# Low parts of the weight tiles in the tail: GpSimd in eight pieces, two tiles on VectorE

## The chip, the cores and the metric

One core of a Trainium2 chip runs the whole program. The time is device microseconds (us) of one execution; the median of several runs is compared. Engines by the profile's names: PE (TensorE, matmuls), DVE (VectorE), ACT (ScalarE), POOL (GpSimd), SP (SyncE, which issues nearly all DMAs).

## The reference

A fused model of two blocks in float32, sequence length 256, width 1024. The first block is one hybrid layer (attention and spatial gating, then 16 experts that choose their tokens) and a norm. The second block has two layers, an even one (sliding-window and latent attention, 8 heads each) and an odd one (16 heads with forget gates, FOX below). Cut to what the tail of the kernel computes:

```
x = rmsnorm(xl + gt2 * expert_choice_ffn(...), g_final)      # end of the first block

def mla_swa_layer(x, positions, g_in, w_in, ...):
    h = rms_norm(x, g_in)
    z = h @ w_in
    cq, ckv, kpe, q_s, k_s, v_s, gate = split_cols(z, EVEN_SPLITS)
    ...                                    # 8 latent heads, 8 sliding-window heads
    o = jnp.concatenate([o_mla, o_swa], axis=-1)
    return x + (o * jax.nn.silu(gate)) @ w_out

def fox_layer(x, g_in, w_in, b_f, w_out):
    h = rms_norm(x, g_in)
    q, k, v, f_logit, gate = split_cols(h @ w_in, ODD_SPLITS)
    ...                                    # 16 heads, causal, with cumulated log gates
    return x + (o * jax.nn.silu(gate)) @ w_out
```

## The kernel before

The program is one core's list of instructions per engine, in the order in which the code is written (a manual schedule); each engine runs its list in that order, and waits where an instruction needs another engine's result.

**Weights and slots.** A weight tile is 128 x 2048 float32 (1 MB): 256 columns of a weight matrix, with the eight blocks of 128 rows (k = 0 to 7) side by side, 256 columns each. The tiles lie in a fixed number of slots of SBUF. `get(i)` gives tile i, `done(i)` frees its slot, and each freed slot makes `pump()` (L254) issue the next load on SP, in one fixed order.

**Split products.** In the tail every product is made of three matmuls on float32r operands, `mm3` (L141 to L145): high by high, high by low, low by high. `split(i, n, eng, parts)` (L154 to L167) makes the two parts of a weight tile: ScalarE casts the tile (hi, L162), and GpSimd (G) or VectorE (V) subtracts, lo = t − hi (L163). Tables of letters say which engine takes which tile: `ORD_SPLITS` for the five input tiles k, c, v, q and r, `TAIL_SPLITS` for all others of the tail. In the tail GpSimd has c, q, r, all four tiles each of the even layer's gates (g) and output weights (o), and eight of the FOX layer's tiles. Its instruction is one per tile; q's is in two halves, c is 1664 wide.

**End of the first block.** While the last expert's second product runs, `ORD` interleaves it with the input tiles of the even layer, and `stats` collects sums of squares into p_st. Then come the inverse norms on VectorE: ms4 and r4 by L1459 to L1462 and `rsqrt` (L180 to L192: an integer estimate and three Newton steps), and rr at L1464. After that a string, `REST = "cBqtQ"`, sets the order: `latent_out` (c), then for B two `bc_rows` (TensorE spreads a column over the partitions into p_bc, L1340, and VectorE copies it, L1342) and `keys_out` (L1478, L1481), then q's product is finished (q), a transpose (t), and `q_out(0)` (Q, L1499), which scales the first queries. `q_out(1)` for tile r runs inside the pipeline.

**The attention pipelines.** `pipeline` runs over pairs of heads, 4 sliding-window and 4 latent ones: `soft_a` makes the scores (p_s) and the exponentials (L1361 on VectorE, L1365 on ScalarE), `soft_n` divides (`V.tensor_scalar`, L1380, four per pair), `soft_b` transposes (p_pt, L1387; copies L1390 and L1392), `soft_c` multiplies with the values and gates the result (og L1445, ogh L1446, ogl L1447). A table `fills` puts other work between these: the gate products (p_gate, L1436 to L1439), the transposes p_hT (L1602), the splits of the g and o tiles (`ESP` sets their places), and `eo_part`, the output product (p_eo), for the tiles o0 to o3. The odd layer has a second such pipeline over 8 pairs with its own fills (k scaled at L1762, bias L1841, p_oo).

Of the kernel before, what the change touches and what calls it, by code (L numbers as in the profile page):

```python
# [14 lines left out]
OP = mybir.AluOpType  # L15
# [14 lines left out]
ORD_SPLITS = "VGVGG"  # L30
# [6 lines left out]
PARTS = (1, 1, 2, 2, 1)  # L37
# [25 lines left out]
def body(ctx, tc, x, c, ctx_in, c_ctx, w_mod, b_mod, g_mix, g_ffn, w_in, q_gain, k_gain, v_gain,  # L63
# [4 lines left out]
    PE, V, S, G = nc.tensor, nc.vector, nc.scalar, nc.gpsimd  # L68
# [16 lines left out]
    def slot(name, weight=False):  # L85
        if not weight:
            keep[0] = max(keep[0] - 1, 0)
        if not slots_free:
            raise RuntimeError("slots: " + " ".join(v[3] for v in owner.values()))
        n = next((n for n in slots_free if weight or n not in slow), slots_free[0])  # L90
        slots_free.remove(n)
        slow.discard(n)
        t = big.tile([128, 2048], F32, name=name, tag="B%d" % n)
        owner[id(t)] = (slots_free, n, t, name)
        return t
# [14 lines left out]
    def free(*ts):  # L110
        for t in ts:
            q, n, _, _ = owner.pop(id(t))
            q.append(n)
        pump()
# [14 lines left out]
    def small(name, shape, dt=F32, bufs=2):  # L129
        return work.tile(list(shape), dt, name=name, tag="sm_" + name, bufs=bufs)  # L130
# [4 lines left out]
    def mm(o, lhsT, rhs, start, stop):  # L135
        PE.matmul(o, lhsT, rhs, start=start, stop=stop, skip_group_check=True)  # L136

    def r_(ap):
        return ap.bitcast(F32R)
# [14 lines left out]
    def split(i, n=2048, eng=None, parts=1):  # L154

        t = get(i)
        hi, lo = slot("hi"), slot("lo")
        if eng is None:
            eng = dict(G=G, V=V)[TAIL_SPLITS[i - qup_i + 5]]
        for a in range(parts):  # L160
            c_ = slice(n * a // parts, n * (a + 1) // parts)
            S.copy(r_(hi[:, c_]), t[:, c_])  # L162
            eng.tensor_tensor(r_(lo[:, c_]), t[:, c_], hi[:, c_], op=OP.subtract)  # L163
        if i >= qup_i:
            limit[0] = max(limit[0], i + AHEAD[i - qup_i + 5])
        done(i)
        return hi, lo  # L167
# [82 lines left out]
    def pump(upto=-1):  # L250
        while len(tiles) <= min(limit[0], len(loads) - 1) and len(slots_free) > (0 if len(tiles) <= upto else keep[0]):
            t = slot("w%d" % len(tiles), True)
            for view, src in loads[len(tiles)]:
                nc.sync.dma_start(view(t), src)  # L254
            tiles.append(t)

    def get(i):
        if i >= len(tiles):
            limit[0] = max(limit[0], i)
            pump(i)  # L260
        return tiles[i]

    def done(*idx):
        free(*[tiles[i] for i in idx])
# [43 lines left out]
    e_i, E_COLS = {}, {"k": 928, "q": 416, "r": 672}  # L308
    for e in range(NEXP):
# [7 lines left out]
        else:  # L317
            for ch in ORD:
# [6 lines left out]
                else:  # L325
                    n, a2 = int(ch) // 2, int(ch) % 2
# [211 lines left out]
    W = {}  # L538
# [29 lines left out]
    for nm, g in (("q", qg), ("k", kg)):  # L568
        t = small("rows_" + nm, (128, 256), bufs=1)
# [8 lines left out]
    qr = qr_.rearrange("p (b h a d) -> p b h a d", b=2, h=8, a=2)  # L578
# [359 lines left out]
    for m2 in range(4):  # L938
        w = W.pop("o%d" % m2)
# [157 lines left out]
    def between(e):  # L1097

        def f(z, k):
            if z == 1 and k == 0 and e == 0:  # L1100
                index_columns()
                hold(6)
                tables()
            if z == 1 and e + 1 < NEXP and k in (2, 4, 6):
                (pick, fetch, turn)[k // 2 - 1](e + 1)
        return f


    def hidden(e):

        hp, xe, before = [], xes.pop(e), between(e)
        for z in range(2):
            p = bank("p_h%d" % z)
            for k in range(8):
                before(z, k)
                t = get(exp_i[e][z][k]).rearrange("p (a j m) -> p a j m", a=4, j=4)
                lhs = xe[:, 32 * k:32 * k + 32]
                for j in range(4):
                    mm(p[32 * j:32 * j + 32, :].rearrange("p (a m) -> p a m", a=4), lhs, t[:, :, j, :], k == 0, k == 7)
                done(exp_i[e][z][k])  # L1120
            hp.append(p)
        s1 = w2k("s1")
        S.activation(s1, hp[0], AF.Silu)
        hid = w2k("hid")
        V.tensor_tensor(hid, s1, hp[1], op=OP.mult)  # L1125
        free(*hp)
        hidT = w2k("hidT").rearrange("p (a s) -> p a s", a=16)
        for a in range(4):
            V.transpose(hidT[:, 4 * a:4 * a + 4, :], hid[:, 128 * a:128 * a + 128].rearrange("p (r q) -> p q r", q=4))  # L1129
        oh4 = w2k("oh4", 256)  # L1130
        V.tensor_scalar(r_(oh4), trow, ig4[:, e:e + 1], None, op0=OP.is_equal)
        return hidT, oh4
# [111 lines left out]
    def freer(key):  # L1244
        return lambda: free(*W.pop(key))

    hidT, oh4 = hidden(NEXP - 1)
    sqs = [small("rows_" + c_, (128, 256), bufs=1) for c_ in "qk"]
    steps, accs, reach = deque(), {}, {}
# [35 lines left out]

    for ch in ORD:
        if ch in e_i:
            W[ch] = split(e_i[ch], 1664 if ch in "cv" else 2048, dict(G=G, V=V)[ORD_SPLITS["kcvqr".index(ch)]],
                          PARTS["kcvqr".index(ch)])
            if ch == "v":  # L1290
                if have < 8:
                    more("c")
            elif have < 8:
                product(ch)
            continue
        n, a2 = int(ch) // 2, int(ch) % 2
        if a2 == 0:
            yp = bank("p_y")
        busy(BUSY[int(ch)])
        i = exp_i[-1][2][int(ch)]  # L1300
        t = get(i)
        for z in range(2):
            for q in range(4):
                mm(yp[32 * q:32 * q + 32, 0:256], hidT[:, 8 * a2 + 4 * z + q, :],
                   t[:, 1024 * z + 256 * q:1024 * z + 256 * q + 256], a2 == 0 and z == 0, a2 == 1 and z == 1)
        done(i)
        if a2 == 0:
            some(STEPS[n])
            continue
        ys = gated(NEXP - 1, yp[:, 0:256], 256)  # L1310
        free(yp)
        flush()
        some(STEPS[4 + n])
        p = bank("p_sc")
        for i in range(2):
            for mi in range(2):
                mm(p[:, 256 * mi:256 * mi + 256], r_(ys[i][:, 128 * mi:128 * mi + 128]), r_(oh4),
                   i == 0 and mi == 0, i == 1)
        for mi in range(2):
            m = 2 * n + mi  # L1320
            add_to_x(m, p[:, 256 * mi:256 * mi + 256])
            scaled(y1h[:, m, :], y1l[:, m, :], xT[:, m, :], gfe[:, m:m + 1])
            add_squares(m)
        free(p)
        flush()
        some(STEPS[8 + n])
        have = 2 * n + 2
        for c_ in accs:
            more(c_)
        for m in {2: (5,), 3: (6, 7)}.get(n, ()):  # L1330
            steps.append(lambda m=m: stats(m))
# [5 lines left out]
    def bc_rows(col2, name):  # L1337
        p = bank("p_bc")
        for b in range(2):
            PE.transpose(p[:, 128 * b:128 * b + 128], col2[:, b:b + 1].to_broadcast([128, 128]), ident)  # L1340
        t = small(name, (128, 256), bufs=1)
        V.tensor_copy(t, p[:, 0:256])  # L1342
        free(p)
        return t
# [118 lines left out]
    rsqrt(r4, ms4, 4)  # L1463
    V.tensor_tensor(rr, r4[:, 2:4], r1, op=OP.mult)  # L1464
    free(p_st)
    zt_, qst_ = slot("zt"), slot("qst")
    zn = zt_[:, 0:832].rearrange("p (b n) -> p b n", b=2)
    vsn = zt_[:, 832:1088].rearrange("p (b n) -> p b n", b=2)
# [7 lines left out]
    def keys_out():  # L1476
        p = finish("k")
        V.tensor_tensor(vT, p[:, 256:512], rb, op=OP.mult)  # L1478
        for v_ in range(2):
            for a in range(2):  # L1480
                V.tensor_tensor(ksT[64 * a:64 * a + 64, v_, :], p[64 * v_:64 * v_ + 64, 0:256],  # L1481
                                rb[64 * v_:64 * v_ + 64, :], op=OP.mult)
        free(p)
        freer("k")()
# [19 lines left out]
    for ch in REST:  # L1504
        if ch == "B":
            r1b = bc_rows(r1, "rows_q")
            rb = bc_rows(rr, "rows_k")
            keys_out()
        elif ch == "c":
            latent_out()  # L1510
        elif ch == "q":
            finish("q")
        elif ch == "Q":
            q_out(0)
        elif ch == "r":
            product("r")
            some(3)
        elif ch == "t":
            p = bank("p_vT")
            for b in range(2):  # L1520
                PE.transpose(p[:, 128 * b:128 * b + 128], vT[:, 128 * b:128 * b + 128], ident)
            S.copy(zt_[:, 832:1088], p[:, 0:256])
            free(p)
# [387 lines left out]
    for b in range(2):  # L1911
        ss = s4[:, 2 * b:2 * b + 2]
        v, u, r, y, z, rf = (s2[:, 6 * b + i:6 * b + i + 1] for i in range(6))
# [45 lines left out]
```

## Time and profile before

| | us |
|---|---|
| median of 3 runs | 1377.9 (1374.32 to 1378.91) |
| profiled execution, own time | 1375.06 |
| its span | 1373.3 |
| PE busy | 1082.7 (79%) |
| DVE busy | 466.8 (34%) |
| ACT busy | 266.0 (19%) |
| POOL busy | 113.4 (8%) |

Busy shares are means over the whole span. The first three quarters stream the experts' weights; the input tiles of the even layer, and all that the change is about, come in the last quarter, which is called the tail here. "Idle" and "waits" are read for one engine at a time: the time in which it stands, and the instruction whose end let it go on.

### The profile page before, as it was taken

The numbers are of one execution on the slowest core, as the hardware profiler recorded it, in microseconds if no ns is written. First come the engines' busy times: TensorE is split into PE (matmuls) and PEld (weight loads), VectorE is DVE, ScalarE is ACT, GpSimd is POOL, SyncE is SP. The second block draws the span as 40 slices with busy tenths as digits, with TensorE's granted clock in tenths as the row PEclk, the third lists the DMA queues.
The fourth block names the chain that finished last, engine by engine and source line by source line (L and its number), as shares of the span: only waits on it lengthen the run. The fifth ranks groups of instructions, "written<-read, shape, count | busy, mean of one in ns | idle before, by whom it ended". The sixth has DMA issues, their size and how long they took to land.

```text
span 1373.3 us, 16868 instructions
## 1 busy us (share of the span) xinstructions
PE 1082.7 (79%) x6827; PEld 521.8 (38%) x6827; DVE 466.8 (34%) x1167; ACT 266.0 (19%) x537; POOL 113.4 (8%) x65
## 2 busy tenths in 40 slices
PE   6999987777767777776766767777776979899988
PEld 3875932111211111111111211111120667799887
DVE  3747542111201111121111112111120668867984
ACT  3437310000000000000000000000000536545453
POOL 2000100000000000000000000000000332560420
PEclk9999999997979789897888989788896999999999
DMA  9995799999999999999999999999999952381320
GB/s 374 400 400 229 287 387 426 427 426 426 427 427 426 427 427 427 427 427 427 427 426 427 426 426 427 427 427 427 427 427 408 362 182 82 107 290 64 123 93 32
DMA packets 114685, 482.76 MB, mean 352 GB/s; under 512 B 8010, under 2 KB 61520, under 8 KB 63152
## 3 DMA queue, kind: packets, MB, share of 16 engines
q1 hardware_dynamic: 113504, 479.10, 85.4%
q0 software_dynamic: 848, 2.48, 0.6%
q8 instruction: 54, 0.88, 0.2%
q14 instruction: 23, 0.19, 0.0%
q10 hardware_dynamic: 256, 0.10, 0.0%
HBM read 480.59 MB, written 1.06 MB: 351 GB/s over the span
## 4 chain that ended last, share of the span: by engine, by line
DMA 64%; PE 24%; DVE 9%; ACT 2%; issue 1%; ACTq 0%; SPq 0%; DVEq 0%
DMA w<-in_w_dram 63%; PE p_aT L136 4%; PE p_aN L136 3%; PE p_gate L136 2%; PE p_out L136 2%; PE p_oo L136 2%; PE p_mod L136 1%; PE p_eo L136 1%; PE p_aF L136 1%; DVE pr L1380 1%; PE p_s L136 1%; PE p_o L136 1%; PE p_y L136 1%; DVE pr L1361 1%; DVE lo L163 1%
## 5 line engine op out<-in xcount | busy, mean ns | idle before, releaser
L136 PE MATMUL p_y<-w,hidT 128*32 128x512 f32 (+1 forms) x1088 | 237.9, 628 | 65.8 <-DMA w<-in_w_dram 48.8
L136 PE MATMUL p_h<-w,rows_k 128*32 128x512 f32 x1024 | 177.8, 770 | 87.4 <-DMA w<-in_w_dram 87.4
L136 PE MATMUL p_h<-w,rows_q 128*32 128x512 f32 x1024 | 172.9, 753 | 87.2 <-DMA w<-in_w_dram 85.7
L163 POOL TENSOR_TENSOR lo<-w,hi 128x2048 fp32r<-128x2048 f32 (+2 forms) x20 | 86.7, 4340 | 1005.7 <-DVE hidT L1129 903.9
L136 PEld LDWEIGHTS p_y<-w,hidT 128*32 128x32 f32 x1088 | 54.9, 116 | 253.6 <-issue 144.6
L1139 DVE SCALAR_TENSOR_TENSOR ysl<-p_y,ig,ysh 128x512 fp32r<-128x512 f32 (+1 forms) x34 | 24.4, 719 | 262.1 <-ACT ysh L1138 260.6
L136 PEld LDWEIGHTS p_h<-w,rows_k 128*32 128x32 f32 x1024 | 25.7, 119 | 206.3 <-DMA w<-in_w_dram 178.6
L136 PEld LDWEIGHTS p_h<-w,rows_q 128*32 128x32 f32 x1024 | 25.5, 119 | 201.1 <-DMA w<-in_w_dram 170.5
L1041 DVE TENSOR_SCALAR oh<-p_ix,cst,rs 128x32 f32<-128x32 f32 x30 | 7.9, 306 | 265.9 <-PE p_ix L136 265.9
L1138 ACT ACTIVATE ysh<-p_y,ig 128x512 fp32r<-128x512 f32 (+1 forms) x34 | 22.4, 662 | 388.8 <-PE p_y L136 388.8
L1062 ACT COPY xr<-p_g 64x256 f32<-64x256 f32 x16 | 5.8, 365 | 432.2 <-PE p_g L136 227.7
L162 ACT CAST hi<-w 128x2048 fp32r<-128x2048 f32 (+3 forms) x44 | 75.0, 1729 | 23.6 <-DMA w<-in_e_w_in_dram 19.2
L163 DVE TENSOR_TENSOR lo<-w,hi 128x2048 fp32r<-128x2048 f32 (+2 forms) x24 | 47.7, 2005 | 23.3 <-ACT hi L162 22.1
L1143 DVE SCALAR_TENSOR_TENSOR xT<-p_sc,m,xT 128x256 f32<-128x256 f32 x128 | 51.8, 475 | 4.0 <-PE p_sc L136 4.0
L1125 DVE TENSOR_TENSOR hid<-s,p_h 128x512 f32<-128x512 f32 x16 | 11.0, 687 | 95.0 <-PE p_h L136 95.0
L1063 DVE COPY xr<-p_g 64x256 f32<-64x256 f32 x16 | 6.7, 416 | 94.1 <-ACT xr L1062 94.1
L136 PE MATMUL p_aT<-y2h,hi 128*128 128x256 f32 x128 | 36.7, 287 | 0.0
L136 PE MATMUL p_aT<-y2h,lo 128*128 128x256 f32 x128 | 36.3, 284 | 0.2 <-POOL lo L163 0.2
L136 PE MATMUL p_aT<-y2l,hi 128*128 128x256 f32 x128 | 36.3, 284 | 0.1
L136 PE MATMUL p_g<-yn,oh 128*32 128x512 f32 x128 | 34.6, 660 | 0.4 <-DVE oh L1008 0.4
L1365 ACT ACTIVATE pr<-pr,st 128x128 f32<-128x128 f32 x64 | 28.5, 448 | 32.1 <-DVE st L1361 32.1
L1380 DVE TENSOR_SCALAR pr<-pr,st 128x128 f32<-128x128 f32 x64 | 27.4, 491 | 0.6
(488 smaller groups left out, 1783.4 us busy)
## 6 DMA issues: line engine op xcount, KB each, us to landing
w<-in_w_dram SPq DMA_DIRECT2D x376, 1024.0 KB, 19.6
w<-in_w_mod_dram SPq DMA_DIRECT2D x24, 1024.0 KB, 11.1
w<-in_o_w_in_dram SPq DMA_DIRECT2D x16, 1024.0 KB, 7.8
w<-in_w_dram SPq DMA_DIRECT2D x16, 512.0 KB, 8.0
w<-in_w_in_dram SPq DMA_DIRECT2D x7, 1024.0 KB, 17.3
w<-in_e_w_in_dram SPq DMA_DIRECT2D x7, 1024.0 KB, 9.8
w<-in_w_out_dram SPq DMA_DIRECT2D x4, 1024.0 KB, 9.4
w<-in_e_w_out_dram SPq DMA_DIRECT2D x4, 1024.0 KB, 10.7
```

Source lines behind the costliest of these rows:

```text
L136: PE.matmul(o, lhsT, rhs, start=start, stop=stop, skip_group_check=True)
L162: S.copy(r_(hi[:, c_]), t[:, c_])
L163: eng.tensor_tensor(r_(lo[:, c_]), t[:, c_], hi[:, c_], op=OP.subtract)
L1041: V.tensor_scalar(oh[b], p[:, 0:n], table(C_TCOL + b, 1), rs2[:, b:b + 1], op0=OP.is_equal, op1=OP.mult)
L1063: V.tensor_copy(t[:, 256:512], p[0:64, 256:512])
L1125: V.tensor_tensor(hid, s1, hp[1], op=OP.mult)
L1138: S.activation(r_(h), yp, AF.Copy, scale=g)
L1139: V.scalar_tensor_tensor(r_(l), yp, g, h, op0=OP.mult, op1=OP.subtract)
L1143: V.scalar_tensor_tensor(xT[:, m, :], p, gt2[:, m:m + 1], xT[:, m, :], op0=OP.mult, op1=OP.add)
L1361: V.tensor_tensor_reduce(t[:, c0:c1], sp[:, c0:c1], bb[b], scale, init, OP.add, OP.min, st[:, 2 * z + b:2 * z + b + 1])
L1365: S.activation(t[:, c0:c1], t[:, c0:c1], AF.Exp, bias=st[:, 2 * z + b:2 * z + b + 1], scale=-1.0, accum_out=st[:, 4 + 2 * z + b:5 + 2 * z ...
L1380: V.tensor_scalar(t[:, c0:c1], t[:, c0:c1], st[:, 8 + 2 * z + b:9 + 2 * z + b], None, op0=OP.mult)
```

## The change

In `split`, a tile whose low part is GpSimd's is now subtracted in eight instructions of an eighth of the columns each (256, and 208 for c), so that each is one of the eight k blocks of the tile; VectorE's low parts stay whole. For the last two input tiles, q and r, a new function `split_late` casts both in halves on ScalarE and puts their low parts (two halves each, now VectorE's) and the `done` of the tile into lists. These are called later: q's first half behind rr, its second half and `done` between the two copies of `bc_rows` and `keys_out`, and r's two halves and `done` behind `keys_out`.

```diff
@@ split
-            eng.tensor_tensor(r_(lo[:, c_]), t[:, c_], hi[:, c_], op=OP.subtract)
+            w = n // 8 if eng is G else n // parts
+            for b in range(c_.start, c_.stop, w):
+                d_ = slice(b, b + w)
+                eng.tensor_tensor(r_(lo[:, d_]), t[:, d_], hi[:, d_], op=OP.subtract)
@@ new
+    lows = {"q": [], "r": []}
+
+    def split_late(i, low):
+
+        t, hi, lo = get(i), slot("hi"), slot("lo")
+        for a in range(2):
+            c_ = slice(1024 * a, 1024 * a + 1024)
+            S.copy(r_(hi[:, c_]), t[:, c_])
+            low.append(lambda c_=c_: V.tensor_tensor(r_(lo[:, c_]), t[:, c_], hi[:, c_], op=OP.subtract))
+        low.append(lambda: done(i))
+        return hi, lo
+
@@ for ch in ORD
-            W[ch] = split(e_i[ch], 1664 if ch in "cv" else 2048, dict(G=G, V=V)[ORD_SPLITS["kcvqr".index(ch)]],
-                          PARTS["kcvqr".index(ch)])
+            if ch in "qr":
+                W[ch] = split_late(e_i[ch], lows[ch])
+            else:
+                W[ch] = split(e_i[ch], 1664 if ch in "cv" else 2048, dict(G=G, V=V)[ORD_SPLITS["kcvqr".index(ch)]],
+                              PARTS["kcvqr".index(ch)])
@@ behind rr
     free(p_st)
+    lows["q"].pop(0)()
@@ for ch in REST, "B"
             rb = bc_rows(rr, "rows_k")
+            for f in lows["q"]:
+                f()
             keys_out()
+            for f in lows["r"]:
+                f()
```

The list of VectorE before, from the last step of the inverse norms to the first scaled queries (rs_t and r are the rsqrt's, rows_q and rows_k the spread columns, vT and zt the keys and values, qst the queries):

```order
L191 SCALAR_TENSOR_TENSOR rs_t_5517<-r_5510,rs_u_5516 128x1 x4
L192 SCALAR_TENSOR_TENSOR r_5510<-rs_t_5517,r_5510 128x4
L1464 TENSOR_TENSOR rr<-r_5510 128x2
L1342 COPY rows_q<-p_bc 128x256
L1342 COPY rows_k<-p_bc 128x256
L1478 TENSOR_TENSOR vT<-p_aT,rows_k 128x256
L1481 TENSOR_TENSOR zt<-p_aT,rows_k 64x256 x4
L1499 SCALAR_TENSOR_TENSOR qst<-p_aT,slope,rows_k 128x256 x2
```

The same stretch of VectorE's list after the change (w_5196 is tile q, w_5202 tile r):

```order
L194 SCALAR_TENSOR_TENSOR rs_t_5522<-r_5515,rs_u_5521 128x1 x4
L195 SCALAR_TENSOR_TENSOR r_5515<-rs_t_5522,r_5515 128x4
L1482 TENSOR_TENSOR rr<-r_5515 128x2
L1258 TENSOR_TENSOR lo<-w_5196,hi 128x1024
L1360 COPY rows_q<-p_bc 128x256
L1360 COPY rows_k<-p_bc 128x256
L1258 TENSOR_TENSOR lo<-w_5196,hi 128x1024
L1497 TENSOR_TENSOR vT<-p_aT,rows_k 128x256
L1500 TENSOR_TENSOR zt<-p_aT,rows_k 64x256 x4
L1258 TENSOR_TENSOR lo<-w_5202,hi 128x1024 x2
L1518 SCALAR_TENSOR_TENSOR qst<-p_aT,slope,rows_k 128x256 x2
```

Four low parts of 1024 columns have come in between rr and the first scaled queries; the rest stands as it stood.

GpSimd's list before, from the last sums of squares of the first block on (w_5718, w_5724 and w_5726 are the first tiles of the pipeline, the last line is a small load of the FOX layer's gate weights):

```order
L1242 TENSOR_TENSOR rows_k<-rows_k,sq 128x256
L163 TENSOR_TENSOR lo<-w_5196,hi 128x1024 x2
L163 TENSOR_TENSOR lo<-w_5202,hi 128x2048
L163 TENSOR_TENSOR lo<-w_5718,hi 128x2048
L163 TENSOR_TENSOR lo<-w_5724,hi 128x2048
L163 TENSOR_TENSOR lo<-w_5726,hi 128x2048
L1684 DMA wf<-in_o_w_in_dram 128x8x32
```

And after (w_5727, w_5740 and w_5742 are the same three tiles under new numbers):

```order
L1245 TENSOR_TENSOR rows_k<-rows_k,sq 128x256
L166 TENSOR_TENSOR lo<-w_5727,hi 128x256 x8
L166 TENSOR_TENSOR lo<-w_5740,hi 128x256 x8
L166 TENSOR_TENSOR lo<-w_5742,hi 128x256 x8
L1707 DMA wf<-in_o_w_in_dram 128x8x32
```

q's and r's low parts are gone from GpSimd's list, and each tile behind them is eight instructions; the order of the tiles is the same. The lists of PE and SP keep their order, and ScalarE's has r's cast in two halves.

## Rows read from the trace of the kernel before

**Rows 1.** Busy time by stretch: from:to, length, each engine's busy us, clock, DMA.
```profile
1109.30:1112.30 3.00, 3.00 (x16) 3.00 (x15) 2.87 (x7) 2.16 (x10) 0.00 (x0) 0.50 1.09 385
1200.00:1279.00 79.00, 78.87 (x665) 75.71 (x664) 56.33 (x115) 37.07 (x60) 28.69 (x13) 1.00 0.54 181
```

The columns of this view: us, then busy time of PE, PEld, DVE, ACT and POOL with the count of instructions, the granted clock as a share of full speed, the share of DMA, GB/s.

**Rows 2.** What TensorE waited for in the tail: us in total, times, longest.
```profile
PE p_bc L1340 <- DVE r L192: 7.3, 1, 7.3
PE p_eo L136 <- ACT ogh L1446: 4.8, 1, 4.8
PE p_s L136 <- DVE k L1762: 2.5, 1, 2.5
PE p_pt L1387 <- DVE pr L1380: 2.4, 1, 2.4
PE p_gate L136 <- DVE lo L163: 1.7, 1, 1.7
```

**Rows 3.** The chain of waits round the inverse norms: start us, us, what.
```profile
1097.36 1.81 DVE ms L1462
1099.19 2.32 DVE r L180
1101.58 4.39 DVE r L182
...
1108.54 1.11 PE p_bc L1340 x4
1109.65 7.43 PE p_aT L136 x48
...
1117.64 0.93 PE p_s L136 x8
```

**Rows 4.** VectorE's timeline ahead of these: start us, us, instruction.
```profile
1096.96 0.17 DVE L1460 RECIPROCAL rr<-ms 128x2 f32<-128x2 f32 x1
1097.16 0.16 DVE L1461 SCALAR_TENSOR_TENSOR ms<-rr,p_st 128x2 f32<-128x2 f32 x1
```

**Rows 5.** GpSimd's timeline, with the idle time before and what ended it.
```profile
1082.84 0.73 POOL L1242 TENSOR_TENSOR rows_k<-rows_k,sq 128x256 f32<-128x256 f32 x1
1083.54 0.91 POOL L1242 TENSOR_TENSOR rows_q<-rows_q,sq 128x256 f32<-128x256 f32 x1
1084.40 0.73 POOL L1242 TENSOR_TENSOR rows_k<-rows_k,sq 128x256 f32<-128x256 f32 x1
...
1096.68 9.25 POOL L163 TENSOR_TENSOR lo<-w,hi 128x1024 fp32r<-128x1024 f32 x3 [5.01 <-ACT hi L162]
...
1181.68 9.29 POOL L163 TENSOR_TENSOR lo<-w,hi 128x2048 fp32r<-128x2048 f32 x2 [7.99 <-DVE st L1361]
```

**Rows 6.** VectorE's L1215 beside such a sum, and later without one.
```profile
1082.89 0.96 DVE L1215 SCALAR_TENSOR_TENSOR y1l<-xT,gfe,y1h 128x256 fp32r<-128x256 f32 x1 [0.62 <-ACT y1h L1214]
...
1093.82 0.48 DVE L1215 SCALAR_TENSOR_TENSOR y1l<-xT,gfe,y1h 128x256 fp32r<-128x256 f32 x1 [0.22 <-ACT y1h L1214]
```

**Rows 7.** The chain of waits in the pipelines of both layers.
```profile
1139.45 4.29 DVE pr L1380
...
1145.37 2.83 PE p_hT L1602 x16
...
1152.92 1.88 PE p_hT L1602 x16
...
1193.56 9.21 PE p_eo L136 x56
...
1209.54 5.96 PE p_eo L136 x48
...
1302.04 2.29 DVE lo L163
...
1309.43 6.79 PE p_aN L136 x48
```

**Rows 8.** ScalarE's cast of tile o3 in its timeline.
```profile
1199.36 1.91 ACT L162 CAST hi<-w 128x2048 fp32r<-128x2048 f32 x1 [4.35 <-POOL lo L163]
```

## The prediction

> **What bounds the kernel now.** I first read the table of waits of the matmul engine over the tail [rows 2]. Before the tail the kernel loads the experts' weights, and the change touches nothing there that anybody waits for. In the tail TensorE is the engine to look at: in the 79 us from 1200 it is busy 78.87 us [rows 1], although GpSimd does 28.69 us of low parts beside it. A delay of another engine costs time only where TensorE stands for it, and the table names the five long stands: 7.3, 4.8, 2.5, 2.4 and 1.7 us, 18.7 us together. These, and matmuls that run slower after such a stand, are all that can be won in the tail.
>
> Next I asked the chain of waits what makes DVE late [rows 3]. Three operations on a few elements each take 1.81, 2.32 and 4.39 us: L1462, L180 and L182, all arithmetic from SBUF to SBUF. The reciprocal among them takes 0.17 us and L1461, which reads PSUM, 0.16 [rows 4]. The timeline of GpSimd holds the reason: low parts of the q and r tiles run there from 1096.68 for 9.25 us [rows 5], and the last long DVE operation ends at 1105.97, within 0.05 us of the end of the last of them. An operation of DVE whose data are in SBUF, other than a reciprocal, stands until the GpSimd operation ends. At 1139.45 L1380 takes 4.29 us on the chain [rows 7], which is about the length of one whole tile of GpSimd: two take 9.29 [rows 5].
>
> The Trainium skill, page "SBUF — State Buffer", section "Who interferes with whom", says that DVE and GpSimd share one pair of ports, which one instruction holds exclusively until it ends. The three norm operations agree. The same rule speaks against pieces: a GpSimd operation that already waits may take the ports after every single DVE operation. That is rival A, which is priced from rows below.
>
> **Part 1: the low parts of q and r leave GpSimd and go behind the norms.** Removed: three GpSimd operations, and with them the three stands. At 0.17 us instead of 1.81, 2.32 and 4.39 the norms end 8.52 − 0.51 = 8.0 us earlier. p_bc now starts at 1108.54 [rows 3], and rr is there a moment later, at about 1108.7; then 1100.7. TensorE stood 7.3 us for it [rows 2], so that it can begin p_bc right behind p_lat, at 1101.2. Having stood, it ran the q product (48 matmuls) in 7.43 us [rows 3], while 48 of the same shape later take 5.96 [rows 7]; the granted clock just behind the stand is 0.50 of full speed, the lower level of 1.2 GHz [rows 1]. Without the stand I take 5.96: q would end at 1101.2 + 0.55 (four p_bc at full clock, half their 1.11 us [rows 3]) + 5.96 = 1107.7.
>
> Added on DVE, ahead of the q_out that releases the first attention pair: four halves of 1024 columns. A tile of 2048 takes DVE 2.29 us [rows 7], so a half is 1.15. DVE: rr at 1100.7; q's first half to 1101.85; copies and keys_out (7 operations in 2.87 us [rows 1], the halves between them) and q's second half to 1105.9; r's halves to 1108.2. (TensorE wants q's second half in the middle of the product, at 1104.7; it is there at about 1103.9.) With some 0.1 us for the waits among them q_out begins at 1108.3. Now p_s starts at 1117.64, which is 0.56 us behind the end of the q product at 1109.65 + 7.43 [rows 3]; these 0.56 us are the first half of q_out, so that p_s comes at about 1108.85. TensorE alone would have allowed 1107.7 + 0.56 = 1108.25. So DVE is what ends last here, and the term is **−8.8 us**. The bounds are 0, if something that the trace doesn't show holds q_out, and −9.4. The q tile's weight slot comes free some 2 us later than now, and r's likewise; the loads that take these slots are for tiles of the pipeline that are used much later, so I take nothing for it, and D holds the other case. GpSimd is empty until its next tile, and loses nothing.
>
> **Part 2: eight pieces.** Sixteen tiles of 2048 columns (and c, early, where nobody waits) are written in pieces of 256. Such a piece was already in the trace, as the sums of squares of 128x256: they start 0.70 us apart, and the one beside a DVE operation takes 0.91 [rows 5]. So a tile takes 8 × 0.70 = 5.6 us instead of 4.65, or 8 × 0.87 = 7.0 with a DVE operation in each gap. On the other side L1215 took 0.96 us beside the pieces and 0.48 alone [rows 6]: a stand of half a microsecond where a whole tile would cost four. Nothing else is added: TensorE waits for pieces instead of tiles, which lets it begin on the first of the eight k steps earlier.
>
> What that is worth, stand by stand:
> - p_pt behind L1380: TensorE stood 2.4 us [rows 2], and of the transposes behind it 16 took 2.83 us against 1.88 for as many later [rows 7], so at most 3.35. The four operations of L1380 now each wait for a piece at worst; I take **−2.6**.
> - p_eo behind ogh: 4.8 us [rows 2]. Then 56 matmuls took 9.21 us where 48 at full clock take 5.96, which is 6.95 for 56, so 2.25 us more are in it [rows 7]; at most 7.0. But the lead of GpSimd's queue goes here. It has four tiles in a row, o0 to o3. At 0.75 us a piece, nearer to the lone one, o0 and o1, which start at 1181.68 [rows 5], end 16 × 0.75 = 12.0 us later at 1193.7; o2 at 1199.7; the cast of o3, which stood 4.35 us for o2's low part and takes 1.91 [rows 8], at 1201.6; and the first piece that TensorE wants of o3 is the fifth, at 1205.4. TensorE began o3 at 1209.54 [rows 7] and would now want it 7.0 earlier, at 1202.5, which is 2.9 us too soon. (What parts 1 and this list move before it moves both alike.) I take **−4.0**.
> - p_s behind k (L1762), in the second layer: 2.5 us [rows 2], and the 48 matmuls of p_aN after it 6.79 instead of 5.96 us [rows 7], at most 3.3. DVE meets two whole tiles of GpSimd just before; I take **−2.6**.
> - p_gate behind a low part of DVE: 1.7 us [rows 2]; I take **−1.2**.
> - Elsewhere, as from 1200 to 1279, TensorE has no idle time to give back [rows 1]: 0.
>
> **Sum.** −8.8 − 2.6 − 4.0 − 2.6 − 1.2 = −19.2 us, against the profiled execution's own 1375.06 us: 1355.9. That execution lies 2.84 us below the median of the runs, 1377.9, so I add these: **1358.7 us**.
>
> **Rivals.**
> A. *The engines alternate operation by operation.* Where DVE has one operation after the other in the same place, each may wait for a whole piece. L1215 stood 0.48 us for one; at up to 0.56 us eight pieces stop DVE 4.5 us a tile, as much as one operation does now. For it: a GpSimd piece stretched to 0.91 shows that both engines hand over at each end [rows 5, 6]. Against it: reciprocals and operations on PSUM pass [rows 4], and many of DVE's in these stretches are of this kind. Then only part 1 remains: 1377.9 − 8.8 = 1369.1.
> B. *Everything closes.* All stands and their slow matmuls go: 9.4 + 3.35 + 7.0 + 3.3 + 1.7 = 24.75, so 1353.1. For it: og comes earlier, so that ScalarE's casts do as well. Against it: the queue of o0 to o3 as worked out.
> C. *Slower: GpSimd becomes the bound in o0 to o3.* With a piece every p us, the fifth piece of o3 ends 29p + 1.9 us after the start of o0 (24 pieces, a cast, 5 pieces). TensorE wanted it 27.9 us after it, at 1209.54 − 1181.68. This eats the 8.8 us of part 1 and 4.1 more where 29p + 1.9 = 27.9 + 12.9, from p = 1.34 on, if the other stands also stay; at p = 1.5 it is 1377.9 − 8.8 + 17.5 = 1386.6. The rows have 0.70 alone and 0.87 beside DVE [rows 5]; it would take a DVE operation of 0.6 us in each gap.
> D. *No difference*, within 0.3%, about 4 us, which is roughly what a measurement of this kernel can tell from no change: the halves on DVE or a late load hold q_out by half of what is won, and A holds for the rest: about 1375.
>
> **How the numbers follow.** Part 1 hangs on nothing but removing the three stands, and what DVE has to do instead is priced by operations of the same size; part 2 hangs on how the two engines interleave. I give my forecast 0.53, A 0.22, B 0.15, D 0.05, C 0.05. The forecast, B and nearly all of A are faster by over 0.3%: 0.90 faster, 0.05 the same, 0.05 slower. The range goes from 1349, below B by the scatter of the runs of before, to 1370, just above A; outside are C, D and the edge of A and B.
>
> **What the profile would show.** Part 1 is right if L1462, L180 and L182 take about 0.2 us each, p_bc follows p_lat without a stand, and the first p_s starts some 9 us earlier. If p_s waits for q_out and q_out for r's halves, the order on DVE is the bound, as I say. Part 2 is right if L1380 and L1447 stay under 1 us in a stretch with pieces, and if pieces start 0.7 to 0.9 us apart; A shows as stands of about 0.5 us at nearly every DVE operation there, C as a new wait of p_eo for GpSimd's low part. A wait of p_eo of more than 6 us for o3, or a time over 1370, would make the forecast wrong.

## The result

The changed kernel takes 1355.9 us (median of four runs, 1352.65 to 1357.06) where the kernel before takes 1378.4 beside it: 0.9845 of it, 95% interval 0.982 to 0.9869. The profiled execution took 1356.19 us against 1375.06, 18.9 us less.

Where these 18.9 us lie is read from the matmuls of the two traces. I cut the tail at five of them: the first p_lat of the last, uninterrupted stretch of 24; the first p_s; the end of the first gate product behind the first p_o; the first p_f; the end of the third p_aN product of the odd layer; and the last matmul. The front is all that comes ahead of the first cut. All are us worked out from starts and ends in the traces.

| kernel | front | norms and q: to p_s | first pairs: to gate end | output product: to p_f | odd layer: to p_aN end | rest | whole tail |
|---|---|---|---|---|---|---|---|
| before | 1096.40 | 21.24 | 34.42 | 80.80 | 83.37 | 50.72 | 270.54 |
| changed | 1096.25 | 12.16 | 36.41 | 75.73 | 78.78 | 48.78 | 251.87 |
| difference | −0.15 | −9.08 | **+1.99** | −5.07 | −4.59 | −1.94 | −18.67 |
| forecast | 0 | −8.8 | −2.6 | −4.0 | −2.6 | −1.2 | −19.2 |

The sum came out and one of its terms did not. The waits of TensorE in the tail of the changed kernel show it, beside [rows 2]:

```profile
PE p_hT L1625 <- DVE st L1379: 3.0, 1, 3.0
PE p_eo L136 <- DVE ogl L1465: 1.3, 1, 1.3
...
PE p_s L136 <- DVE qst L1518: 0.7, 1, 0.7
...
PE p_eo L136 <- POOL lo L166: 0.3, 1, 0.3
PE p_pt L1405 <- DVE pr L1398: 0.2, 1, 0.2
```

p_bc, p_s behind k and p_gate are gone from the list, and p_eo stands 1.3 us instead of 4.8. But p_hT, which waited for nothing long before, now stands 3.0. (TensorE "stands" while it waits for another engine.)

VectorE's timeline round the inverse norms (start us, us, instruction) answers to the chain in [rows 3]:

```profile
1096.81 0.17 DVE L1478 RECIPROCAL rr<-ms 128x2 f32<-128x2 f32 x1
...
1097.20 0.17 DVE L1480 TENSOR_SCALAR ms<-ms 128x2 f32<-128x2 f32 x1
1097.40 0.17 DVE L183 TENSOR_SCALAR r<-ms 128x4 int32<-128x4 int32 x1
...
1097.61 0.17 DVE L185 TENSOR_SCALAR r<-r 128x4 int32<-128x4 int32 x1
...
1100.46 1.23 DVE L1258 TENSOR_TENSOR lo<-w,hi 128x1024 fp32r<-128x1024 f32 x1
...
1105.48 2.36 DVE L1258 TENSOR_TENSOR lo<-w,hi 128x1024 fp32r<-128x1024 f32 x2
1107.87 0.88 DVE L1518 SCALAR_TENSOR_TENSOR qst<-p_aT,slope,rows_k 128x256 f32<-128x256 f32 x2
```

The three operations that took 1.81, 2.32 and 4.39 us take 0.17 each, and r's halves are what q_out waits for. The chain has the rest: p_bc directly behind p_lat, at full clock in 0.45 instead of 1.11 us, and p_s at 1108.41 instead of 1117.64.

```profile
1101.04 0.45 PE p_bc L1358 x4
...
1108.41 0.93 PE p_s L136 x8
```

In the odd layer the stretch that answers to the one before p_s behind k is now full of matmuls (busy us of PE, PEld, DVE, ACT, POOL; then PE's granted clock), and p_aN runs in 5.93 us where it took 6.79 [rows 7]:

```profile
1270.00:1300.00 30.00, 30.00 (x257) 27.59 (x256) 28.04 (x86) 19.32 (x49) 18.17 (x24) 1.00 0.26 88
```

### The profile page after: what moved, and what is told of

Read it like the earlier page. It is cut to its first block, busy times and chain, and to the rows that moved or that the text cites. A ratio compares the mean times of both kernels' runs of the same rounds, so it can differ in the third digit from the quotient of the medians.

```text
span 1354.4 us, 16988 instructions
## 1 busy us (share of the span) xinstructions
PE 1077.6 (80%) x6827; PEld 517.7 (38%) x6827; DVE 436.7 (32%) x1171; ACT 266.6 (20%) x538; POOL 128.6 (9%) x181
## 4 chain that ended last, share of the span: by engine, by line
DMA 65%; PE 26%; DVE 4%; POOL 2%; issue 1%; ACT 1%; ACTq 0%; SPq 0%; DVEq 0%; POOLq 0%
DMA w<-in_w_dram 65%; PE p_aT L136 5%; PE p_aN L136 3%; PE p_gate L136 3%; POOL lo L166 2%; PE p_out L136 2%; PE p_oo L136 2%; PE p_mod L136 2%; PE p_s L136 1%; PE p_aF L136 1%; PE p_o L136 1%; PE p_lat L136 1%; PE p_y L136 1%; PE p_busy L136 1%; PE p_h L136 1%
## 5 line engine op out<-in xcount | busy, mean ns | idle before, releaser
L136 PE MATMUL p_h<-w,rows_k 128*32 128x512 f32 x1024 | 174.5, 760 | 90.6 <-DMA w<-in_w_dram 90.6
L166 POOL TENSOR_TENSOR lo<-w,hi 128x256 fp32r<-128x256 f32 (+1 forms) x136 | 102.2, 787 | 981.5 <-DVE hidT L1132 903.9
L162 ACT CAST hi<-w 128x2048 fp32r<-128x2048 f32 (+3 forms) x41 | 71.3, 1758 | 26.6 <-DMA w<-in_e_w_in_dram 19.2
L1398 DVE TENSOR_SCALAR pr<-pr,st 128x128 f32<-128x128 f32 x64 | 30.8, 542 | 0.6
## 6 DMA issues: line engine op xcount, KB each, us to landing
w<-in_w_dram SPq DMA_DIRECT2D x376, 1024.0 KB, 19.6
```

The costliest lines, as they stand in the source:

```text
L166: eng.tensor_tensor(r_(lo[:, d_]), t[:, d_], hi[:, d_], op=OP.subtract)
L1398: V.tensor_scalar(t[:, c0:c1], t[:, c0:c1], st[:, 8 + 2 * z + b:9 + 2 * z + b], None, op0=OP.mult)
```

## The experiments

The first theory was that of the prediction: an operation of VectorE on data in SBUF stands until the GpSimd instruction beside it ends. Its open point was what pieces do where such operations follow one another: let them through, or stop each of them (rival A).

### One part alone: the inverse norms

```diff
-            w = n // 8 if eng is G else n // parts
+            w = n // parts
```

> Only the first part of the change: the low parts of q and r on VectorE behind the inverse norms; every other GpSimd tile in one instruction again. My theory (an operation of VectorE with its data in SBUF stands until the GpSimd instruction beside it ends, and the two parts act in different stretches): the inverse norms run undisturbed and the first p_s starts 9.2 us earlier than in the kernel before, as in the changed one (1117.64 to 1108.41); all later stands come back as in the kernel before, p_pt 2.4, p_eo 4.8, p_s 2.5, p_gate 1.7 us within half a microsecond. So 9 us less than before, about 1369. Rival (what the later stretches gained came from freeing GpSimd of q and r, not from the pieces): these stands stay small as in the changed kernel, and the time is 1357 to 1360.

Measured: 1366.6 us median against 1375.4, a ratio of 0.9926 (0.99 to 0.9952). The stretch to p_s is 12.15 us, as in the changed kernel, and the other four are 34.11, 81.56, 83.39 and 50.76, so that the whole tail is 8.6 us shorter. TensorE's waits are those of [rows 2] again, without p_bc (and with 1.0 us before p_hT, which is new):

```profile
PE p_eo L136 <- ACT ogh L1464: 4.8, 1, 4.8
PE p_pt L1405 <- DVE pr L1398: 2.6, 2, 2.4
PE p_s L136 <- DVE k L1785: 2.5, 1, 2.5
PE p_gate L136 <- DVE lo L166: 1.7, 1, 1.7
```

The first part is worth its 9.1 us by itself, and nothing behind it came from freeing GpSimd of q and r. The rival falls.

### The other part alone: the pieces

```diff
@@ split of the kernel before
-            eng.tensor_tensor(r_(lo[:, c_]), t[:, c_], hi[:, c_], op=OP.subtract)
+            w = n // 8 if eng is G else n // parts
+            for b in range(c_.start, c_.stop, w):
+                d_ = slice(b, b + w)
+                eng.tensor_tensor(r_(lo[:, d_]), t[:, d_], hi[:, d_], op=OP.subtract)
```

> Only the second part: all GpSimd low parts of the tail in eight pieces, q and r still on GpSimd ahead of the inverse norms. My theory (each operation of VectorE waits for one piece, then one piece waits for one operation): the norms have about 19 short operations on data in SBUF and meet 16 pieces about 0.72 us apart, 11.6 us together from 1096.7, so that they end at 1108 to 1109 as in the kernel before, and the first p_s starts within 1 us of 1117.64: pieces gain nothing there. The later stretches go as in the changed kernel (-9.7 us in all behind the first p_s), so the time is about 1368 to 1369. Rival (pieces let a short operation through soon, so that the norms lose only some 0.3 us each time): the norms end at about 1103, the first p_s starts 4 to 6 us earlier, and the time is 1362 to 1365.

Measured: 1363.4 us against 1375.4, 0.991 (0.9885 to 0.9934). The time lies in the rival's range, because the later stretches gained more than the 9.7 us that I had counted (11.0 of tail in all) and because the kernel before took 1375.4 us here, not the 1377.9 that I had counted from; the stretch that decides between the two is the first one. There p_s comes 0.19 us earlier than in the kernel before, counted from p_lat, as the theory said, and not 4 to 6. GpSimd's timeline and VectorE's over the norms say why:

```profile
1096.11 11.10 POOL L166 TENSOR_TENSOR lo<-w,hi 128x256 fp32r<-128x256 f32 x16 [5.00 <-ACT hi L162]
```

```profile
1096.99 0.64 DVE L183 TENSOR_SCALAR r<-ms 128x4 int32<-128x4 int32 x1
...
1097.66 0.67 DVE L185 TENSOR_SCALAR r<-r 128x4 int32<-128x4 int32 x1
1098.37 2.73 DVE L194 SCALAR_TENSOR_TENSOR rs_t<-r,rs_u 128x1 f32<-128x1 f32 x4
1101.13 0.65 DVE L195 SCALAR_TENSOR_TENSOR r<-rs_t,r 128x4 f32<-128x4 f32 x1
1101.81 2.69 DVE L194 SCALAR_TENSOR_TENSOR rs_t<-r,rs_u 128x1 f32<-128x1 f32 x4
1104.54 0.65 DVE L195 SCALAR_TENSOR_TENSOR r<-rs_t,r 128x4 f32<-128x4 f32 x1
...
1107.59 0.16 DVE L1467 TENSOR_TENSOR rr<-r 128x2 f32<-128x2 f32 x1
```

Four operations on one column each take 0.61 us in the changed kernel and 2.7 here, one piece of 0.69 us each (11.10 / 16). Hardly any gets past without waiting. So rival A holds wherever short operations on SBUF data follow one another: sixteen pieces stop them for as long as three instructions did. This is why the change had to take q and r away from GpSimd there. Behind p_s the stretches are 35.26, 75.68, 78.78 and 48.78 us; the last three agree with the changed kernel's within 0.1 us. The two parts alone give −8.6 and −11.0 us of tail, 19.6 together, against 18.7 (and 20.1 in the second profile below) for both.

### The term that failed: tile g3

In the changed kernel the row of normalisation and rotation meets the eight pieces of g3 (the timeline of GpSimd has them from 1129.70, 5.68 us long):

```profile
1129.87 0.18 DVE L1395 RECIPROCAL st<-st 128x4 f32<-128x4 f32 x1
1130.09 2.64 DVE L1398 TENSOR_SCALAR pr<-pr,st 128x128 f32<-128x128 f32 x4
1132.65 0.69 DVE L626 TENSOR_TENSOR rp<-zt,SS 128x16 f32<-128x16 f32 x1
1133.27 0.16 DVE L628 TENSOR_TENSOR rp<-zt,SS 128x16 f32<-128x16 f32 x1
1133.35 0.72 DVE L630 TENSOR_TENSOR kp<-zt,CC 128x32 f32<-128x32 f32 x1
1134.10 0.65 DVE L631 TENSOR_TENSOR kp<-kp,rp 128x32 f32<-128x32 f32 x1
1134.79 0.75 DVE L1603 COPY kn<-kp 128x256 f32<-128x256 f32 x1
1135.46 0.16 DVE L626 TENSOR_TENSOR rp<-zt,SS 128x16 f32<-128x16 f32 x1
```

Again nearly every operation waits for one piece, and the row gets fast when the pieces are over. The first test makes g3 one instruction again and leaves the rest.

```diff
-            w = n // 8 if eng is G else n // parts
+            w = n // 8 if eng is G and i != eg_i[3] else n // parts
```

> The changed kernel, but the low part of the one gate tile g3, which meets the second pair's normalisation (L1398) and the rotation of the latent key (L626 to L631), in one GpSimd instruction. My theory (eight pieces stop a row of such operations for as long as one whole instruction does): VectorE ends this row within 1 us of where it ends it in the changed kernel, measured from the recipe of the sums (RECIPROCAL) to the last L1603, 6.5 us; TensorE's stand of 3.0 us before p_hT becomes one of about 2.4 before p_pt, and the end of the first p_gate behind it comes 1 to 2 us earlier than in the changed kernel, since the slow clock then falls on transposes. Total 1 to 2 us less than the changed kernel. Rival (pieces help here as well and the loss is from elsewhere): the row takes over 8 us or the stand grows to 4 us and more, and the total is 1 to 3 us more.

Measured: 1352.2 us in one run. The first pairs take 34.02 us, 2.4 less than in the changed kernel (1.1 less than in its second profile below; I had said 1 to 2), and the other stretches are the changed kernel's. The row, from the end of the reciprocal to the end of the last L1603, takes 6.7 us (1128.49 to 1135.16) against 6.3 in pieces. One instruction puts the whole delay into the first operation, as in the kernel before:

```profile
1128.52 5.00 DVE L1398 TENSOR_SCALAR pr<-pr,st 128x128 f32<-128x128 f32 x4
1133.44 0.16 DVE L626 TENSOR_TENSOR rp<-zt,SS 128x16 f32<-128x16 f32 x1
```

The pieces therefore gained next to nothing here and moved the stand. In the changed kernel p_pt hardly waits, TensorE goes on to p_hT, and there it stands 3.0 us for a bank of PSUM (the memory that matmuls write to) that is freed behind L1379, which is queued behind the whole row on VectorE. It then runs what follows at a lower clock (chain of waits of the changed kernel, beside 0.80 for p_o and 3.06 for a gate product in the kernel before):

```profile
1137.48 1.09 PE p_hT L1625 x4
1138.57 1.48 PE p_o L136 x8
1140.05 4.77 PE p_gate L136 x24
```

With g3 whole, TensorE stands 2.4 us before p_pt and another 1.0 before p_hT, no less in sum. But the lower clock, which I had expected on the transposes, did not come at all. The busy times over the first pairs show both (the kernel before, the changed one, g3 whole; length first, then PE's busy time, and the last but two is the granted clock):

```profile
1117.64:1152.06 34.42, 30.46 (x188) 23.36 (x188) 25.84 (x91) 19.07 (x50) 9.12 (x2) 0.95 0.10 32
1108.41:1144.82 36.41, 31.81 (x188) 23.99 (x188) 25.75 (x92) 19.17 (x50) 11.27 (x16) 0.91 0.34 116
1106.87:1140.89 34.02, 29.20 (x188) 21.77 (x188) 25.49 (x91) 18.78 (x49) 10.15 (x9) 1.00 0.36 124
```

TensorE is idle for 3.96, 4.60 and 4.82 us. So the whole tile's 2.4 us against eight pieces are slower matmuls and not less waiting.

The second test leaves the pieces and takes them out of the row.

```diff
-ESP = (1, 8, 19, 27, 38, 40, 46, 48, 55)
+ESP = (1, 9, 19, 27, 38, 40, 46, 48, 55)
```

> The changed kernel with the split of gate tile g3 put behind the latent key's and value's products in the same step of the pipeline, so that its eight pieces start some 2.5 us later and lie beside operations of VectorE that read PSUM. My theory: the four L1398 and the first rotation take about 1.0 and 0.9 us instead of 2.6 and 2.8, the stand of 3.0 us before p_hT falls under 1 us, the gate product behind it runs at full clock (3.1 instead of 4.8 us), and the first pair of gate products ends 3 to 5 us earlier than in the changed kernel; some of it may come back as a wait of p_eo for o3's pieces. Total 2 to 5 us less than the changed kernel, 1351 to 1354. Rival (the stand is set by the bank that p_hT waits for, whatever GpSimd does): the stand stays at 2 us and more and the total is within 1 us of the changed kernel.

Measured: 1351.4 us against 1375.4, 0.9824 (0.98 to 0.9847); the first pairs take 31.41 us, 5.0 less than in the changed kernel, and all behind them is as there. Most of the row is free, and its end still meets three pieces, which leaves 1.1 us of the stand:

```profile
1129.71 1.01 DVE L1398 TENSOR_SCALAR pr<-pr,st 128x128 f32<-128x128 f32 x4
...
1131.84 0.60 DVE L631 TENSOR_TENSOR kp<-kp,rp 128x32 f32<-128x32 f32 x1
1132.48 0.76 DVE L1603 COPY kn<-kp 128x256 f32<-128x256 f32 x1
1133.16 0.95 DVE L1687 SCALAR_TENSOR_TENSOR xT<-xT,smT,rows_q 128x256 f32<-128x256 f32 x1
1134.04 0.34 DVE L1379 CUSTOM_DVE_ANT_0 pr<-p_s,distm,nsink 128x128 f32<-128x128 f32 x1
```

L1379, which reads PSUM, takes 0.34 us here as everywhere, with pieces running beside it. I had expected less than 1 us of the stand; the rest of the expectation held. So the last test of this kind moves g3 once more, behind the gate product g4.

```diff
-ESP = (1, 8, 19, 27, 38, 40, 46, 48, 55)
+ESP = (1, 13, 19, 27, 38, 40, 46, 48, 55)
```

> The changed kernel with the split of gate tile g3 one step of the pipeline later still, behind the first gate product (g4). My theory: its eight pieces then meet neither the rotation of the latent key nor L1687, which lost 0.4, 0.5 and 0.5 us to them with the split behind the value's products; the stand of 1.1 us before p_hT falls to 0.3 us or less, and the first gate product ends up to 1 us earlier than there. The pieces now lie beside the next pair's normalisation (four L1398), which TensorE wants some 4 us later, so nothing is lost: the stretch from the start of p_lat to the end takes 245.7 to 246.7 us against 246.7. Rival (moved pieces only move the stand): p_pt waits 1 us and more for L1398 and the stretch takes 248 us and more.

Measured: 1351.0 us against 1375.7, 0.9817 (0.9801 to 0.9834). The stand before p_hT is gone from the list of waits, the first pairs take 30.06 us (1.3 less, where I had said up to 1), and the tail 245.59, 0.1 below the range that I gave. The next normalisation does not hold p_pt, but not for the reason that I gave: its four L1398 took 1.01 us from 1138.14, and the pieces began only at 1139.88, behind it. In the tail this is the shortest of all versions, 6.3 us less than the changed kernel's first profile and 4.9 less than its second; against the version before it the medians differ by less than their scatter.

### The size of a piece

The diff is that of `w`, with n // 2, n // 4 and n // 16 in place of n // 8.

> The changed kernel with GpSimd's low parts in two pieces of 1024 columns instead of eight of 256. From the whole tile (4.56 us) and the lone piece (0.70 us) I work out 0.15 us a piece and 2.15 ns a column, so a piece of 1024 takes some 2.35 us. My theory (an operation of VectorE on data in SBUF waits for the piece beside it, so that the loss is the smaller of pieces met times their length and the number of such operations times it): the rows with few such operations between reads of PSUM lose up to 2.35 us at a time; the stand of p_eo grows from 1.3 to some 3 us and one of the later stands (p_s behind k, p_gate) partly returns. Total 3 to 7 us more than the changed kernel. Rival (any division is enough, since TensorE has slack for one piece): within 1.5 us of the changed kernel.

> The changed kernel with four pieces of 512 columns, some 1.25 us each, 5.0 us a tile. My theory: the row of normalisation and rotation ends as before, since eight or four pieces stop it for as long as a whole tile; TensorE waits a little more for ogl (2 us instead of 1.3), and o3 is there sooner (third of four pieces 20.7 us after the start of o0 instead of 23.4), so that this 0.3 us wait goes; the odd layer stays closed. Total within 1.5 us of the changed kernel. Rival (only short pieces help): 3 us or more lost.

> The changed kernel with sixteen pieces of 128 columns, some 0.43 us each alone, 6.8 us a tile. My theory: GpSimd's queue becomes the bound for the output product: o3's tenth piece comes 58 x 0.43 + 1.9 = 26.8 us after the start of o0 instead of 23.4, so that a wait of p_eo for GpSimd of 2 to 4 us appears; VectorE's operations stand 0.2 to 0.4 us each, more often. The odd layer stays closed. Total 2 to 4 us more than the changed kernel. Rival (the shorter the lock, the better): the row of normalisation and rotation ends 1 us and more earlier, p_eo waits less than 1 us in all, and the total is 1 to 2 us less.

Measured, one run each: 1362.4, 1358.4 and 1360.2 us. The tails, in the columns of the first table:

| pieces | to gate end | to p_f | to p_aN end | rest | whole tail |
|---|---|---|---|---|---|
| 1 (first part alone) | 34.11 | 81.56 | 83.39 | 50.76 | 261.96 |
| 2 | 34.04 | 78.10 | 82.87 | 50.06 | 257.22 |
| 4 | 33.72 | 77.40 | 78.99 | 50.26 | 252.51 |
| 8 (changed) | 36.41 | 75.73 | 78.78 | 48.78 | 251.87 |
| 16 | 34.45 | 81.94 | 78.78 | 48.78 | 256.11 |

Two pieces lose 5.4 us to eight, inside what I expected: p_eo stands 4.0 us, p_s behind k all its 2.5 again, and p_gate 1.0. Four pieces lose 0.6, within the expectation (2.1 against the changed kernel's second profile below, which is not), but the parts don't hold: p_eo stands 3.3 us (I had said 2), p_gate 1.2 (I had said that the odd layer stays closed), and the first pairs give back 2.7. Sixteen lose 4.2, just above the upper end, and by the mechanism that was named, the wait for GpSimd in the output product, which is larger than the 2 to 4 us expected:

```profile
PE p_eo L136 <- POOL lo L166: 5.4, 7, 2.3
```

o0 to o2 take 21.11 us there against 17.76 with eight pieces. So eight is near the best of these sizes for the stretches where operations on SBUF and on PSUM mix. In the row of normalisation and rotation no size helps much: between one and sixteen pieces its stretch stays within 33.7 and 36.4 us, of which TensorE is idle for 3.4 to 4.9, while moving the tile brings 30.1, with 1.4 idle. The other part of the differences between the sizes in this stretch is matmuls at the lower clock (mean granted clock 0.91 to 1.00).

### The changed kernel and the moved tile on one chip

> The changed kernel once more, beside the next one on the same chip. My theory (the scatter of the runs comes from ahead of the tail; the tail itself repeats): from the start of p_lat's last stretch to the end the profile takes 251.9 us again, within 0.3 us, and the time is 18 to 23 us less than before. Rival (the scatter is in the tail): this stretch moves by a microsecond or more.

> The changed kernel with the split of gate tile g3 behind the latent key's and value's products, again, beside the changed kernel. My theory: 5 us less than the changed kernel, all of it up to the first pair of gate products; the tail takes 246.7 us from the start of p_lat's last stretch, within 0.3 us. Rival (the earlier difference was the scatter of the runs): within 2 us of the changed kernel.

Measured: 1354.1 us (1353.33 to 1355.43), a ratio of 0.9852 (0.9838 to 0.9865), and 1351.1 (1346.75 to 1351.84), 0.9814 (0.9797 to 0.983), so 3 us between the medians where I had said 5, with no run of the one among the other's; the tails differ by 3.7 us, all of it in the first pairs. The moved tile's tail repeated, 246.76 against 246.73 us. The changed kernel's did not as expected: 250.45 instead of 251.87, so that here the rival was right. 1.3 of these 1.4 us lie in the first pairs, where the stand of 3.0 us was the same but the clock came back sooner (busy time by stretch; the last but two is the granted clock; the changed kernel, then its second profile, each over its gate product):

```profile
1140.00:1144.80 4.80, 4.80 (x28) 4.66 (x26) 2.71 (x8) 1.34 (x3) 0.00 (x0) 0.60 0.00 0
```

```profile
1138.60:1142.10 3.50, 3.50 (x27) 3.37 (x26) 2.71 (x8) 1.34 (x3) 0.00 (x0) 0.86 0.00 0
```

The changed kernel thus loses 0.7 to 2.0 us in the first pairs, and the price of the clock behind one and the same stand differs by more than a microsecond from one execution to the next.

## Why the prediction held, and where it failed

**Norms and q: −9.1, forecast −8.8.** Every step is in the trace: three stands less, p_bc at 1101 behind p_lat, q at full clock, and VectorE's halves as the last thing before q_out. A half takes 1.23 us, but the next operation starts 1.14 us after it, where I had 1.15; q_out began at 1107.87, forecast 1108.3.

**First pairs: forecast −2.6, measured +2.0 (+0.7 in the second profile).** This is the step that failed: "The four operations of L1380 now each wait for a piece at worst". They did, 2.64 us for four instead of 1.0. But eleven more operations on SBUF data stand behind them in the same row (L626 to L1603 twice, then L1687). Four of these waited for the other four pieces, and TensorE's next need lay behind all of them: the bank for p_hT, freed behind the scores' operation (L1379) at the row's end. So the stand of 2.4 us became one of 0.2 and one of 3.0. I had priced the first operation that TensorE waited for and not the queue behind it. Rival A had the mechanism of this row right and its price nearly (no gain). Of the 2.0 us, 0.6 are idle time and 1.4 slower matmuls; that the lower clock would fall on a gate product rather than on transposes was in neither. Why it fell for twice as long in the one profile as in the other, and not at all with g3 whole, is not shown.

**Output product: −5.1, forecast −4.0 out of at most 7.0.** This is where the pieces did what they were meant to do. In the kernel before, ogl met a whole tile and the next four L1380 another; in the changed kernel ogl met one piece (0.41 us alone):

```profile
1182.43 4.15 DVE L1447 TENSOR_TENSOR ogl<-og,ogh 128x256 fp32r<-128x256 f32 x1
...
1187.49 4.29 DVE L1380 TENSOR_SCALAR pr<-pr,st 128x128 f32<-128x128 f32 x4
```

```profile
1172.53 0.98 DVE L1465 TENSOR_TENSOR ogl<-og,ogh 128x256 fp32r<-128x256 f32 x1
...
1175.78 2.70 DVE L1398 TENSOR_SCALAR pr<-pr,st 128x128 f32<-128x128 f32 x4
```

GpSimd's queue came as worked out, which these lines of its timeline and ScalarE's show (0.74 us a piece, forecast 0.75; o3's cast behind o2's last piece):

```profile
1171.79 17.76 POOL L166 TENSOR_TENSOR lo<-w,hi 128x256 fp32r<-128x256 f32 x24 [6.12 <-issue]
...
1191.56 13.63 POOL L166 TENSOR_TENSOR lo<-w,hi 128x256 fp32r<-128x256 f32 x16 [2.02 <-ACT hi L162]
```

```profile
1189.58 1.90 ACT L162 CAST hi<-w 128x2048 fp32r<-128x2048 f32 x1 [7.34 <-POOL lo L166]
```

TensorE came to o3 23.7 us after the start of o0, where I had 20.8, because it had first stood 1.3 us for ogl, and because its first p_eo came 6.4 us after the start of o0 where in the kernel before it came 4.3 us after it: I had taken both to move alike. So o3's pieces were just in time, and the wait for them is 0.3 us instead of 2.9. Behind o3 p_aT now waits 0.6 us for y2h, which I had not counted. That GpSimd's queue is only just fast enough is what sixteen pieces showed.

**Odd layer −4.6 and rest −1.9, forecast −2.6 and −1.2, bounds 3.3 and 1.7.** Both bounds were too low. For the odd layer that was an arithmetic fault: to the stand of 2.5 us I added the slow p_aN and left out the p_s ahead of it, which is slowed as well (1.61 us instead of 0.93), and an idle time of 0.2 us. For p_gate no matmul ran at the lower clock: the 24 of its product took 3.39 us besides the stand of 1.7, against 3.13 in the changed kernel, and I had taken 1.2 of the 1.7 without a reason. The pieces don't make VectorE's rows there quick either (four L1398 take 2.63 us at 1274.63, as in the first pairs), but reads of PSUM lie between, and TensorE had other products to do in the meantime.

**The total.** That the sum of the terms is half a microsecond from the tail's 18.7 is luck: the first pairs' 4.6 us of error and 4.1 us of errors the other way nearly cancel. What holds by itself is the first term. The median lies 2.8 us below the forecast of 1358.7, which is the offset that I added: the profiled execution of before lay 2.84 us under the median shown with it, and that of the changed kernel lies within 0.3 us of its median.

The rule on the shared ports ("SBUF — State Buffer" of the Trainium skill, section "Who interferes with whom") agrees with the traces here in what it says of one instruction: the norms' operations of 0.64 to 0.67 us above end within 0.05 us of the end of a piece. It says who waits, and the runs add that the turn changes after nearly every instruction. What waited here is of the kinds that it names, two inputs in SBUF (L626 to L631) or a copy or tensor_scalar (L1603, L1398), which "on data in SBUF" above stands for; the reciprocal, with one input, took 0.18 us beside a piece. That a read of PSUM passes is in L1379's 0.34 us beside pieces.

## What to carry to other kernels

Where VectorE stands behind a GpSimd instruction on SBUF data, count the operations of the same kind that follow in its queue before dividing the instruction: one isolated operation gains almost the whole length (4.15 us became 0.98), four in a row gain a part (4.29 became 2.70), and a row with as many operations as there are pieces gains next to nothing, because nearly each waits for a piece. For a row, take the GpSimd work away, in time or to another engine; that cost one number in a table here and was worth more in its stretch than any size of piece. And price a stand by what the waiting engine wants next behind it in the same queue, and by the clock at which it starts again.

## What the hardware showed beyond that

- GpSimd's subtraction of 128 x n float32 in SBUF fits 0.15 us and 2.15 ns a column through 4.56 us for 2048 and 0.70 for 256 (alone, start to start); 16 pieces of 128 took 6.80 us by that rule's 6.8, four of 512 took 4.98.
- VectorE and GpSimd took turns nearly one for one: 16 pieces in 11.10 us with a short VectorE operation let through after each, now and then two (L183 and L184), so that GpSimd lost nothing and VectorE ran about one operation per 0.69 us.
- After a stand of 2.4 us before p_pt the granted clock of TensorE was 0.56 over the six p_pt in the kernel before, and 1.00 over the same six after the same stand with the first part alone and with g3 whole. What decides it is not shown here.
- The scatter of the profiled executions comes mostly from ahead of the tail: in twelve profiles the front took 1094.7 to 1101.6 us whatever the kernel, while the stretch to p_s repeated within 0.02 us in all ten that have the first part. The tail of the changed kernel moved by 1.4 us between its two profiles.
